# Hybrid decoder step: value products, modulation products and inverse blocks issued as one group each, bias tables made by one product, one mask a tile of probabilities, gates transposed a block at a time

## The chip, the cores and the metric

The kernel runs on one core of one Trainium2 chip. The time is the device time of one execution in microseconds (us); the number given for a kernel is the median of several runs. A profiled execution gives the spans and waits; its own time stands beside its span below. Engines are named as in the profile: PE is TensorE (matmul), PEld its weight loads, DVE VectorE, ACT ScalarE, POOL GpSimd, SP SyncE, which here issues almost all DMAs.

## The reference

One step of a hybrid decoder layer for a prompt of 2048 tokens and eight samples of 8 tokens, model width 1024. One input projection feeds two mixers; their outputs are joined, projected back and added to the input, and a gated feed-forward part follows. The parts that the change touches:

```python
mod = jnp.einsum('bd,de->be', jax.nn.silu(c), w_ada[i]) + b_ada[i]     # six vectors of 1024
sh1, sc1, g1, sh2, sc2, g2 = jnp.split(mod[:, None, :], 6, axis=-1)
h = _rmsnorm(x, norm_mix_w[i]) * (1 + sc1) + sh1
proj = jnp.einsum('bld,de->ble', h, w_in[i])
qkv, z, b_raw, a_raw, sq, sk, sv = _split_cols(proj, IN_SPLITS)
...
# gated DeltaNet, per chunk: T is the inverse of (A + I), A strictly lower triangular
beta = sigmoid(b_raw); g = -exp(A_log) * softplus(a_raw + dt_bias)
...
# sliding window attention, 8 heads, window 128, blocks of 128 queries and 256 keys
s = q k^T * 64 ** -0.5 + rel_bias[_t5_bucket(dist)]       # where 0 <= dist < 128
p = exp(s - m) / (sum(exp(s - m)) + exp(sink - m))
o = p @ v                                                 # keys of the block before and of this one
```

For a query block of 128, key j of the block before is inside the window only where j > i, and key j of the same block only where j <= i. So of the 256 probabilities of a row exactly 128 can differ from zero, and the kernel holds both halves in one 128x128 tile per head.

## The kernel before, in words

Matrices lie with channels on the 128 partitions and tokens along the free dimension. The big projections are done with weights and activations each split into a high and a low fp32r part, three products for one; the products of the mixers are plain float32, which the chip runs as two instructions each. The program runs these stages:

1. Start: the first modulation vectors, the norm of the first half of the tokens, the first products.
2. First input projection (`inproj(0, ...)`, `in_ps`) with a list of small tasks laid beside it: the other modulation vectors (`ada_cols`, L171 on, `ada_ps`), the bias tables (`bias_tables`, L532 on, `toep_ps`), the gates (`gates`, L449 on, `ba_ps` and `bat_ps`), norms of the second half, sums of down-projection weights.
3. The first half's mixers, chunk by chunk of 128 tokens (`mixers(0, ...)`): for each chunk the DeltaNet front part (`front`), the inverse (`levels`, L806 on, `z_ps` and `u_ps`), the state scan (`scan`) and the attention (`attend`, L970 on). Beside them the second half's input projection runs as filler.
4. Output projection and the feed-forward up projection of the first half (`op_ps`, `up_ps`), then the second half's mixers with the up projection as filler, then the sample group.
5. The rest of the feed-forward part (`uq_*`) and the down projection (`dn_ps`), some 1100 us, whose code the diff leaves alone.

The order of work: steps are generators, and `beside(steps, filler, share)` runs `share` steps of the filler for each small step. That fixes the order in which the program is traced. A scheduler with a timing model of its own then places the instructions of each engine, taking the earliest traced first where operands are ready by its model. On the chip each engine runs its list in that order. `tc.issue_after(x)` binds the instructions of a block on x's engine to stand behind x in it.

What the change touches:

- `ada_cols`: for four tiles of 128 columns, each a load of 512 KB (`wada`, six buffers) and eight matmuls on a quarter of the array's columns each, into one PSUM bank (L177 to L182).
- `gates`: for each block of up to 512 tokens, `ba_ev` is transposed 128 tokens at a time (L470), and each transposed piece is reduced at once (L471), 17 pairs in all.
- `bias_tables`: for each of eight heads, one matmul of the bias vector, repeated 128 times, with a one-hot table (L543), a copy (L545) and a store of 128 equal rows to `toep` (L546).
- `levels`: the first level's 16 products `z_ps` of 32x32 blocks (L815 to L817), one for each of four heads and four diagonal blocks. A block's matmul uses its own 32 rows and columns of the array. The blocks of `T` come by four DMAs, one a block.
- `attend`: the probabilities of four heads (`nl`) are transposed (L1023), copied by ScalarE to `pt` (L1025) and multiplied on POOL by two masks (L1028), into a tile for the block before (`C_TGT`) and one for this block (`C_TLE`). Four products (L1033) then sum both halves for the two value heads `v`, which take 64 columns of the array each. The first chunk has no block before it and makes two products.
- `early_h` borrows buffers of the mixers by their tags (L244).

## Time and profile before

| | |
|---|---|
| median of 3 runs | 2617.37 us (2616.8 to 2622.02) |
| the profiled execution's own time | 2613.15 us |
| its span in the profile | 2611.2 us |
| mean granted clock of TensorE | 0.998 |
| PE, PEld busy | 98%, 85% |
| DVE, ACT, POOL busy | 71%, 49%, 31% |
| DMA | 427.62 MB, mean 164 GB/s |

Busy times are unions: while two matmuls overlap, the time counts once. In the profile a group of instructions is named by line, engine, operation and tiles, "out<-in". A row of the timeline has the start, the length, engine, line and tiles, and xN where equal instructions in a row are merged. Matmuls overlap their neighbours, so the cost of one is read from its start to the start of the next one.

### The profile page before, as it was taken

To read this page: it belongs to the slowest core of one execution; us is meant where nothing else is said; L and a number is where in the kernel's file an instruction comes from. 1 tells how busy PE (TensorE), PEld (TensorE's weight loads), DVE (VectorE), ACT (ScalarE), POOL (GpSimd) and SP (SyncE) were. 2 spreads that over 40 slices of the span, in tenths; PEclk is the share of its full clock that TensorE was granted. 3 is DMA by queue.
4 is the path that set the end of the run, shared out by engine and by line. 5 is a ranking of instruction groups with operands and counts; after the bars stand their busy time and mean duration, and the time that the engine had idled before them with its cause. 6 is when DMAs were issued, how large, how long until landed. Compare 5 with 4: busy or idle time off the path is not lost.

```text
span 2611.2 us, 45384 instructions
## 1 busy us (share of the span) xinstructions
PE 2546.3 (98%) x16424; PEld 2213.2 (85%) x16424; DVE 1841.7 (71%) x3632; ACT 1290.2 (49%) x3139; POOL 802.5 (31%) x712
## 2 busy tenths in 40 slices
PE   6999999999999999999999999999999999999998
PEld 5677888888888787777777789999999998888998
DVE  6375579897543687888768674886777677687676
ACT  5464365554343454455444353554555554454453
POOL 2064243334232422223121123335655520021022
PEclk9999999999999999999999999999999999999999
DMA  7787554343556353343336357424555548676454
GB/s 275 252 293 265 154 152 118 104 116 91 126 172 207 112 154 85 98 110 95 90 107 207 122 192 221 139 69 157 172 169 179 181 146 299 206 248 200 141 191 136
DMA packets 315820, 427.62 MB, mean 164 GB/s; under 512 B 82211, under 2 KB 206212, under 8 KB 315332
## 3 DMA queue, kind: packets, MB, share of 16 engines
q1 hardware_dynamic: 315308, 423.61, 51.1%
q8 instruction: 129, 2.11, 0.3%
q0 software_dynamic: 288, 1.11, 0.1%
q14 instruction: 95, 0.78, 0.1%
HBM read 305.07 MB, written 120.57 MB: 163 GB/s over the span
## 4 chain that ended last, share of the span: by engine, by line
PE 76%; DVE 9%; DMA 7%; POOL 3%; issue 2%; ACT 2%; SPq 1%; POOLq 0%; DVEq 0%; ACTq 0%
PE up_ps L365 19%; PE dn_ps L1834 17%; PE in_ps L365 12%; PE op_ps L365 4%; PE uq_b L1616 4%; PE uq_c L1616 2%; PE uq_u L1616 2%; PE uq_g L1616 2%; PE pv_ps L1033 1%; DVE ev L573 1%; PE uq_a L1616 1%; PE as_ps L996 1%; PE u_ps L811 1%; DMA rawu<-in_w_upT_dram 1%; PE z_ps L811 1%
## 5 line engine op out<-in xcount | busy, mean ns | idle before, releaser
L365 PE MATMUL in_ps<-hi,w_hi 128*128 128x512 f32 (+2 forms) x880 | 317.7, 364 | 5.5 <-DVE ev L629 2.4
L365 PE MATMUL up_ps<-hi,w_hi 128*128 128x512 f32 (+2 forms) x808 | 314.5, 389 | 1.5 <-ACT sg L568 1.5
L365 PE MATMUL in_ps<-lo,w_hi 128*128 128x512 f32 (+2 forms) x880 | 313.8, 357 | 1.8 <-DVE lo L297 1.5
L365 PE MATMUL up_ps<-lo,w_hi 128*128 128x512 f32 (+2 forms) x808 | 313.3, 388 | 1.9 <-DVE lo L297 1.9
L365 PE MATMUL in_ps<-hi,w_lo 128*128 128x512 f32 (+2 forms) x880 | 314.2, 357 | 0.0
L365 PE MATMUL up_ps<-hi,w_lo 128*128 128x512 f32 (+2 forms) x808 | 311.6, 386 | 0.0
L1834 PE MATMUL dn_ps<-tl,wh 128*128 128x512 f32 (+2 forms) x796 | 271.5, 341 | 0.0
L1834 PE MATMUL dn_ps<-th,wh 128*128 128x512 f32 (+2 forms) x796 | 269.9, 341 | 0.0
L1834 PE MATMUL dn_ps<-th,wl 128*128 128x512 f32 (+2 forms) x796 | 268.8, 341 | 0.0
L357 DVE TENSOR_TENSOR w_lo<-w_raw,w_hi 128x1024 fp32r<-128x1024 f32 x115 | 145.0, 1261 | 86.1 <-ACT w_hi L356 81.2
L356 ACT CAST w_hi<-w_raw 128x1024 fp32r<-128x1024 f32 x126 | 132.1, 1048 | 139.9 <-PE op_ps L365 55.5
L365 PEld LDWEIGHTS in_ps<-hi,w_hi 128*128 128x128 f32 x880 | 165.1, 188 | 31.4 <-issue 8.6
L365 PEld LDWEIGHTS up_ps<-lo,w_hi 128*128 128x128 f32 x808 | 152.4, 189 | 37.3 <-issue 10.7
L365 PEld LDWEIGHTS in_ps<-lo,w_hi 128*128 128x128 f32 x880 | 165.5, 188 | 21.2 <-issue 3.8
L365 PEld LDWEIGHTS up_ps<-hi,w_hi 128*128 128x128 f32 x808 | 152.1, 188 | 35.8 <-issue 8.6
L365 PEld LDWEIGHTS in_ps<-hi,w_lo 128*128 128x128 f32 x880 | 165.3, 188 | 17.8 <-issue 3.6
L365 PEld LDWEIGHTS up_ps<-hi,w_lo 128*128 128x128 f32 x808 | 152.2, 188 | 31.3 <-issue 5.3
L1718 ACT CAST wh<-wr 128x512 fp32r<-128x512 f32 x149 | 92.3, 619 | 158.9 <-PE dn_ps L1834 105.0
L573 DVE SCALAR_TENSOR_TENSOR ev<-rb,cw,ev 128x512 f32<-128x512 f32 (+2 forms) x180 | 141.1, 789 | 38.9 <-ACT ev L566 35.5
L1834 PEld LDWEIGHTS dn_ps<-tl,wh 128*128 128x128 f32 x796 | 150.5, 189 | 15.3
L1834 PEld LDWEIGHTS dn_ps<-th,wl 128*128 128x128 f32 x796 | 150.5, 189 | 15.3
L1834 PEld LDWEIGHTS dn_ps<-th,wh 128*128 128x128 f32 x796 | 150.2, 189 | 15.4
(569 smaller groups left out, 6520.6 us busy)
## 6 DMA issues: line engine op xcount, KB each, us to landing
w_raw<-in_w_upT_dram SPq DMA_DIRECT2D x50, 512.0 KB
wada<-in_w_ada_dram SPq DMA_DIRECT2D x48, 512.0 KB
w_raw<-in_w_inT_dram SPq DMA_DIRECT2D x44, 512.0 KB
wr<-ws_d SPq DMA_DIRECT2D x88, 256.0 KB
w_raw<-in_w_outT_dram SPq DMA_DIRECT2D x34, 512.0 KB
d<-act_d SPq DMA_DIRECT2D x33, 512.0 KB
wr<-in_w_downT_dram SPq DMA_DIRECT2D x66, 256.0 KB
proj<-ev SPq DMA_DIRECT2D x44, 256.0 KB
```

What stands on the lines that cost most here:

```text
L356: nc.scalar.copy(hi, raw)
L357: (eng or nc.vector).tensor_tensor(lo, raw, hi.bitcast(F32), ALU.subtract)
L365: nc.tensor.matmul(ps[:, :n], a[:, k, :], b[:, k, :n], start=first is not False and k == ks[0] and i == 0, stop=last is not False and k == ...
L573: nc.vector.scalar_tensor_tensor(out, src(j), w[:, j:j + 1], out, ALU.mult, ALU.add)
L811: mm = lambda out, a, b, r, c: nc.tensor.matmul(out, a, b, start=True, stop=True, tile_position=(r, c))
L996: nc.tensor.matmul(banks[v][:, 256 * g:256 * g + 256 - P * k0], qs[:, 2 * (g0 + g) + v], t[:, v, :2 - k0].rearrange("p w j -> p (w j)"), s ...
L1033: nc.tensor.matmul(pv_ps[64 * v:64 * v + 64, :], (vprev[0], vt)[half][:, 64 * v:64 * v + 64], PT[v, half], start=half == k0, stop=half == 1)
L1616: nc.tensor.matmul(bk[t][:, :nb], u[:, k], v[:, k], start=new and k == 0 and y == 0, stop=k == KG - 1 and y == 2, skip_group_check=True)
L1718: nc.scalar.copy(h, raw)
L1834: nc.tensor.matmul(acc[m, s][:, :n], w[q, i][a][:, c], th[b][:, v], start=new and i == 0 and y == 0, stop=i == KH - 1 and y == 2, skip_gro ...
```

## The change

- `ada_cols`: where a group's weights aren't loaded yet, all four loads are issued first, and the products run from the last tile to the first. A new helper `behind` binds all later matmuls of the group behind its first.
- `gates`: all transposes of a block go to one PSUM bank, side by side; one reduction takes the whole tiles of a block, one more the short last tile.
- `bias_tables`: the bias vectors of eight heads are repeated 16 times each instead of 128 times, so one matmul gives 16 equal rows for every head; one copy; each store writes every row eight times.
- `levels`: the first level's products run from the last block to the first within a head, all bound behind the first one written.
- `attend`: the tile for the block before is not masked. The sum over both blocks is written as unmasked probabilities times the old values plus the probabilities masked by `C_TLE` times the difference of new and old values (`dv`, made on POOL). So POOL does one multiply a tile and one small subtraction a chunk. The four products are written from this block to the one before and from value head 1 to 0, bound behind the first. The buffers are two `pt` and two `PT` instead of one and four, and one `he` for the difference.

```diff
+    def behind(latest):
+        return tc.issue_after(latest[0]) if latest else nullcontext()
...
         ps = bank("ada_ps")
-        for q, (comp, kt) in enumerate(tiles):
-            wt = loaded[q] if loaded else ada_load(comp, kt, wpool)
+        latest = []
+        wts = loaded or [ada_load(*t, wpool) for t in tiles]
+        for q in range(len(tiles)) if loaded else range(len(tiles) - 1, -1, -1):
             for k in range(KT):
                 g = k % 4
-                nc.tensor.matmul(ps[32 * g:32 * g + 32, P * q:P * q + P], cT[:, k, :], wt[:, k, :],
-                                 start=k < 4, stop=k >= 4, tile_position=(0, 32 * g))
+                with behind([] if loaded else latest):
+                    mm = nc.tensor.matmul(ps[32 * g:32 * g + 32, P * q:P * q + P], cT[:, k, :], wts[q][:, k, :],
+                                          start=k < 4, stop=k >= 4, tile_position=(0, 32 * g))
+                latest.append(mm.ins)
...
-            for t in range(0, n, P):
+            for i, t in enumerate(range(0, n, P)):
                 rows = min(P, n - t)
-                nc.tensor.transpose(ps[:rows, t:t + 32], ev[:32, t:t + rows], cst[:32, C_ID:C_ID + 32])
-                nc.vector.tensor_reduce(ba[:rows, j, :], ps[:rows, t:t + 32].rearrange("p (a r) -> p r a", r=16)[:, 0:8],
-                                        mybir.AxisListType.X, ALU.add)
-                j += 1
+                nc.tensor.transpose(ps[:rows, 32 * i:32 * i + 32], ev[:32, t:t + rows], cst[:32, C_ID:C_ID + 32])
+            for i, m, rows in ((0, n // P, P), (n // P, 1, n % P)):
+                if rows:
+                    v = ps[:rows, 32 * i:32 * i + 32 * m].rearrange("p (j a r) -> p j r a", a=2, r=16)[:, :, 0:8]
+                    nc.vector.tensor_reduce(ba[:rows, j:j + m, :], v, mybir.AxisListType.X, ALU.add)
+                    j += m
...
-        rx = pool.tile([33, 8, P], F32, tag="relx", name="relx")
+        rx = pool.tile([33, 8, P // 8], F32, tag="relx", name="relx")
...
+        ps = bank("toep_ps", "sc")
+        nc.tensor.matmul(ps[:, :TOEP], rx.rearrange("p h r -> p (h r)"), oh, start=True, stop=True)
+        ev = gw.tile([P, 512], F32, tag="cv", name="toep_ev", bufs=CV)[:, :TOEP]
+        nc.scalar.copy(ev, ps[:, :TOEP])
         for h in range(8):
-            ps = bank("toep_ps", "sc")
-            nc.tensor.matmul(ps[:, :TOEP], rx[:, h, :], oh, start=True, stop=True)
-            ev = gw.tile([P, 512], F32, tag="cv", name="toep_ev", bufs=CV)[:, :TOEP]
-            nc.scalar.copy(ev, ps[:, :TOEP])
-            nc.sync.dma_start(toep[h], ev)
+            rows = slice(P // 8 * h, P // 8 * h + P // 8)
+            nc.sync.dma_start(toep[h].rearrange("(a r) j -> r a j", a=8), ev[rows].unsqueeze(1).broadcast_to([P // 8, 8, TOEP]))
             yield True
...
         z = flat(st_bank("z_ps"), 16)
+        latest = []
         for h in range(H):
-            for g, r in enumerate(blk):
-                mm(z[r, 0, h], AT[r, h, r], diag[g][:, h, 0:BS], 32 * g, 32 * g)
+            for g, r in reversed(list(enumerate(blk))):
+                with behind(latest):
+                    latest.append(mm(z[r, 0, h], AT[r, h, r], diag[g][:, h, 0:BS], 32 * g, 32 * g).ins)
...
+        tle = cst[:, C_TLE:C_TLE + P].unsqueeze(1).broadcast_to([P, 4, P])
+        if not k0:
+            dv = pool.tile([P, 4, P], F32, tag="he", name="dv", bufs=1)[:, 0]
+            nc.gpsimd.tensor_tensor(dv, vt, vprev[0], ALU.subtract)
...
-            pt = pool.tile([P, 4, P], F32, tag="pt", name="pt", bufs=1)
-            nc.scalar.copy(pt, heads(pt_ps))
-            for half in range(k0, 2):
-                PT[v, half] = pool.tile([P, 4, P], F32, tag="PT", name="PT", bufs=4)
-                nc.gpsimd.tensor_tensor(PT[v, half], pt, tri[half], ALU.mult)
+            PT[v, 0] = pool.tile([P, 4, P], F32, tag="pt", name="pt", bufs=2)
+            PT[v, 1] = pool.tile([P, 4, P], F32, tag="PT", name="PT", bufs=2)
+            nc.scalar.copy(PT[v, 0], heads(pt_ps))
+            nc.gpsimd.tensor_tensor(PT[v, 1], PT[v, 0], tle, ALU.mult)
             yield True
         pv_ps = bank("pv_ps", "at")
-        for half in range(k0, 2):
-            for v in range(2):
-                nc.tensor.matmul(pv_ps[64 * v:64 * v + 64, :], (vprev[0], vt)[half][:, 64 * v:64 * v + 64],
-                                 PT[v, half], start=half == k0, stop=half == 1)
+        latest = []
+        for half in range(1, k0 - 1, -1):
+            for v in (1, 0):
+                with behind(latest):
+                    mm = nc.tensor.matmul(pv_ps[64 * v:64 * v + 64, :],
+                                          (vprev[0], vt if k0 else dv)[half][:, 64 * v:64 * v + 64],
+                                          PT[v, half], start=half == 1, stop=half == k0)
+                latest.append(mm.ins)
```

The order that the scheduler writes, at three places. On PE in the second chunk of the first half's mixers, the kernel before; pv_ps are the value products, in_ps is the filler's projection and u_ps belongs to the inverse:

```order
L365 MATMUL in_ps<-hi,w_lo 128x384
L1033 MATMUL pv_ps<-PT,vt 64x512
L365 MATMUL in_ps<-hi,w_hi 128x384
...
L1033 MATMUL pv_ps<-PT,vt 64x512 x2
L365 MATMUL in_ps<-lo,w_hi 128x384
...
L1033 MATMUL pv_ps<-PT,vt 64x512
L811 MATMUL u_ps<-inv_2253,Y 32x32 x8
```

On PE in the same chunk of the changed kernel, where dv is the difference of values and pt the unmasked tile:

```order
L373 MATMUL in_ps<-lo,w_hi 128x384
L1050 MATMUL pv_ps<-PT,dv 64x512 x2
L1050 MATMUL pv_ps<-pt,vt 64x512 x2
L373 MATMUL in_ps<-hi,w_lo 128x384
L373 MATMUL in_ps<-hi,w_hi 128x384
```

The four products stood at three places with filler between them and stand at one now.

On PE in the kernel before, the inverse's first level of a later chunk (z_ps; uu_ps is a product of the scan, as_ps scores of the attention):

```order
L365 MATMUL in_ps<-hi,w_hi 128x384
L811 MATMUL z_ps<-T_2255,AM 32x16
L871 MATMUL uu_ps<-vb,inv_2254 128x128
L811 MATMUL z_ps<-T_2255,AM 32x16
L871 MATMUL uu_ps<-vb,inv_2254 128x128
L811 MATMUL z_ps<-T_2255,AM 32x16
L871 MATMUL uu_ps<-vb,inv_2254 128x128
L811 MATMUL z_ps<-T_2255,AM 32x16 x13
```

On PE in the changed kernel, the same level of the same chunk:

```order
L373 MATMUL in_ps<-hi,w_hi 128x384
L884 MATMUL uu_ps<-vb,inv_2220 128x128 x4
L1012 MATMUL as_ps<-kh,qs 128x256
L1012 MATMUL as_ps<-kl,qs 128x256
L822 MATMUL z_ps<-T_2221,AM 32x16 x16
L1012 MATMUL as_ps<-kh,qs 128x256
```

The 16 block products stood in four pieces between the scan's products and stand in one piece behind them.

On PE in the kernel before, a stretch of the first projection; ada_ps are modulation products, toep_ps bias products, ba_ps and bat_ps belong to the gates, and adat_ps are transposes of modulation vectors:

```order
L365 MATMUL in_ps<-hi,w_hi 128x512
L181 MATMUL ada_ps<-wada,cT 32x128 x6
L543 MATMUL toep_ps<-oh,relx 128x384
L181 MATMUL ada_ps<-wada,cT 32x128 x25
L543 MATMUL toep_ps<-oh,relx 128x384
L181 MATMUL ada_ps<-wada,cT 32x128
L365 MATMUL in_ps<-lo,w_hi 128x512
```

On PE in the changed kernel, the group of modulation products that stands nearest to it, and the gates' transposes of one block:

```order
L373 MATMUL in_ps<-hi,w_lo 128x512
L188 MATMUL ada_ps<-wada,cT 32x128 x32
L373 MATMUL in_ps<-hi,w_hi 128x512
L373 MATMUL in_ps<-lo,w_hi 128x512
L373 MATMUL in_ps<-hi,w_lo 128x512
L478 MATMUL bat_ps<-cst,ba_ev 128x32 x4
```

A group of 32 is in one piece, no bias product stands inside it, and the four transposes of a block follow each other. Counted over the whole order, unbroken runs of pv_ps go from 39 to 17, of z_ps from 73 to 49, of ada_ps from 29 to 19, of bat_ps from 17 to 5, and of toep_ps from 8 to 1.

More of the change, by code (lines that the diff above doesn't have):

```diff
@@ L6 @@
-from contextlib import ExitStack
+from contextlib import ExitStack, nullcontext
 import numpy as np
@@ L244, in early_h @@
         room = iter(spare("xz") + spare("qs", 1, 2) + spare("kh") + spare("kl") + spare("u") + spare("o")
-                    + spare("nl", 3) + spare("nl", 3) + spare("nl", 3) + spare("pt") + [spare("PT", 4)[0] for _ in range(4)])
+                    + spare("nl", 3) + spare("nl", 3) + spare("nl", 3) + [spare(t, 2)[0] for t in ("pt", "pt", "PT", "PT")] + spare("he"))
         for i, t in enumerate(room):
@@ L536, in bias_tables @@
         nc.sync.dma_start(rb[0:32], I["rel_bias"])
[L537 removed]
+        rx = pool.tile([33, 8, P // 8], F32, tag="relx", name="relx")
         oh = pool.tile([33, TOEP], F32, tag="oh", name="oh")
         nc.sync.dma_start(oh, I["consts"][:33, C_OH:C_OH + TOEP])
[L540 to L546 removed]
+        nc.vector.tensor_copy(rx, rb.unsqueeze(2).broadcast_to([33, 8, P // 8]))
+        ps = bank("toep_ps", "sc")
+        nc.tensor.matmul(ps[:, :TOEP], rx.rearrange("p h r -> p (h r)"), oh, start=True, stop=True)
+        ev = gw.tile([P, 512], F32, tag="cv", name="toep_ev", bufs=CV)[:, :TOEP]
+        nc.scalar.copy(ev, ps[:, :TOEP])
+        for h in range(8):
+            rows = slice(P // 8 * h, P // 8 * h + P // 8)
+            nc.sync.dma_start(toep[h].rearrange("(a r) j -> r a j", a=8), ev[rows].unsqueeze(1).broadcast_to([P // 8, 8, TOEP]))
             yield True
@@ L985, in attend @@
         yield True
-        tri = [cst[:, t:t + P].unsqueeze(1).broadcast_to([P, 4, P]) for t in (C_TGT, C_TLE)]
+        tle = cst[:, C_TLE:C_TLE + P].unsqueeze(1).broadcast_to([P, 4, P])
+        if not k0:
+            dv = pool.tile([P, 4, P], F32, tag="he", name="dv", bufs=1)[:, 0]
+            nc.gpsimd.tensor_tensor(dv, vt, vprev[0], ALU.subtract)
         nl = [pool.tile([P, 4, P], F32, tag="nl", name="nl", bufs=3) for _ in range(2)]
```

1 line of the change is left out of this document (removed).

## The prediction

> **What bounds the kernel now.** I read the page first, for busy times and the chain, then the table of busy time by stage, then the timeline of TensorE at the places that the change touches, and last the waits. In the page, look at PE's share, at the granted clock, and at who holds the chain.
>
> ```profile
> span 2611.2 us, 45384 instructions
> PE 2546.3 (98%) x16424; PEld 2213.2 (85%) x16424; DVE 1841.7 (71%) x3632; ACT 1290.2 (49%) x3139; POOL 802.5 (31%) x712
> PEclk9999999999999999999999999999999999999999
> PE 76%; DVE 9%; DMA 7%; POOL 3%; issue 2%; ACT 2%; SPq 1%; POOLq 0%; DVEq 0%; ACTq 0%
> ```
>
> TensorE is busy for 2546.3 of 2611.2 us, idle for 64.9; the granted clock reads 9, 90% or more, in every slice. In the table by stage (length, then busy time of PE, PEld, DVE, ACT, POOL, then clock and DMA share), the start loses 20 us of that and the rest is nearly gapless:
>
> ```profile
> 0.00:65.00 65.00, 44.73 (x410) 33.86 (x411) 44.14 (x110) 33.59 (x59) 14.41 (x15) 1.00 0.77 276
> 65.00:196.00 131.00, 127.76 (x993) 94.50 (x992) 74.28 (x113) 70.79 (x156) 43.32 (x35) 1.00 0.76 272
> 392.00:588.00 196.00, 194.44 (x1648) 172.44 (x1647) 173.49 (x523) 112.92 (x393) 64.69 (x67) 1.00 0.40 113
> 979.00:1371.00 392.00, 387.99 (x2841) 302.50 (x2840) 308.19 (x797) 198.32 (x607) 97.22 (x83) 1.00 0.36 98
> ```
>
> So time taken off TensorE between 65 and 1371 us comes off the end, as long as VectorE (173.5 of 196 us in the first mixer stage) and DMA (share 0.76 in the first projection) keep up. After the sample group's mixers the two kernels issue the same rows in the same order; that part only moves forward. The prediction is a sum of TensorE time, in terms of "visits": a visit is an unbroken run of matmuls of one PSUM tile.
>
> **Value products.** One chunk of attention before, on TensorE (start, length, line, tiles; x4 is two products, since each float32 product is two instructions):
>
> ```profile
> 438.50 0.33 PE L365 MATMUL in_ps<-hi,w_lo 128*128 128x384 f32 x1
> 438.67 0.34 PE L365 MATMUL in_ps<-hi,w_hi 128*128 128x384 f32 x1
> 438.94 1.08 PE L1033 MATMUL pv_ps<-PT,vt 128*64 128x512 f32 x4
> 439.95 0.45 PE L365 MATMUL in_ps<-lo,w_hi 128*128 128x384 f32 x1
> 440.23 0.34 PE L365 MATMUL in_ps<-hi,w_lo 128*128 128x384 f32 x1
> ...
> 440.87 1.07 PE L1033 MATMUL pv_ps<-PT,vt 128*64 128x512 f32 x2
> 441.87 0.35 PE L811 MATMUL u_ps<-inv,Y 32*32 32x32 f32 x10
> ```
>
> A later chunk with three products in one visit, and the weight loads of all visits (min, median, max in ns):
>
> ```profile
> 702.18 1.93 PE L1033 MATMUL pv_ps<-PT,vt 128*64 128x512 f32 x6
> 704.04 0.41 PE L365 MATMUL in_ps<-hi,w_hi 128*128 128x320 f32 x1
> ```
>
> ```profile
> L1033 PEld LDWEIGHTS pv_ps<-PT,vt x124: 132/136/137, 385.4 to 1336.4; 128*64 128x64 f32 x124
> ```
>
> Lengths overlap, so cost is from start to next start. Two products for the two halves of the array cost 1.01 us (438.94 to 439.95), one alone 1.00 (440.87 to 441.87): the second rides free. Three in one visit, a pair and one, cost 1.86, so what follows without a break adds 0.85. A chunk before is mostly alone, pair, alone: 3.01 us in three visits. The changed order has all four in one visit, two pairs: 1.01 + 0.01 + 0.85 = 1.87. Before has 39 visits: nine chunks of three, five of two (1.00 + 1.86), one with its four products in one visit but in the order alone, pair, alone (1.01 + 2 x 0.85 = 2.71), and the first chunk, whose two products follow each other (1.00 + 0.85) and now pair (1.01). Gain: 9 x 1.14 + 5 x 0.99 + 0.84 + 0.84 = 16.9 us.
>
> A rule speaks against the 1.87: the Trainium skill, "TensorE: Matmul & The Clock Gate", Part 3, The mechanism, says that a weight load overlaps running matmuls only where the row group differs, and all four products use all rows. By it the second pair would wait for two loads of 0.136 us, 0.27 a chunk, and the sum would be 4.1 us smaller over 15 chunks. The visit of three has just such a follower, and its 0.85 holds whatever the loads cost; a solitary product, loads and array change included, costs 1.00. So the trace gives no room for 0.27 more, and the 0.85 stands.
>
> **Breaks.** The same rows price a break of the projection's stream. Its matmuls of 384 columns start 0.17 us apart (438.50, 438.67). The last one ahead of the visit takes 0.27 until the visit starts, the first one behind it 0.28 (439.95 to 440.23): 0.10 + 0.11 = 0.21 us beyond the visit's own time. From the order of the two kernels, visits fall from 39 to 17 (pv_ps), 73 to 49 (z_ps), 29 to 19 (ada_ps), 17 to 5 (bat_ps), 8 to 1 (toep_ps): 75 fewer. All at 0.2 make 15.0 us. Where a visit stood among other small products, leaving it restores no stream; if that held for all 36 of z_ps and bat_ps, 39 would be left and 7.8 us. In the chunk shown next the extra visits do break the stream. I take 13, ends 8 and 15.
>
> **Inverse blocks.** z_ps of the first level, in four visits and, in another chunk, in one:
>
> ```profile
> 674.00 0.23 PE L811 MATMUL z_ps<-T,AM 32*32 32x16 f32 x2
> 674.16 0.44 PE L365 MATMUL in_ps<-hi,w_lo 128*128 128x384 f32 x1
> ...
> 676.48 0.42 PE L811 MATMUL z_ps<-T,AM 32*32 32x16 f32 x26
> 676.83 0.44 PE L365 MATMUL in_ps<-lo,w_hi 128*128 128x384 f32 x1
> ```
>
> ```profile
> 468.88 0.44 PE L811 MATMUL z_ps<-T,AM 32*32 32x16 f32 x32
> 469.25 0.44 PE L365 MATMUL in_ps<-lo,w_hi 128*128 128x384 f32 x1
> ```
>
> Three of 0.16 and one of 0.35 against 0.37: 0.46 us for three visits less, 0.15 each; 24 visits make 3.7 us. Ends: 2.5 (some small visits hold two products already) and 3.7.
>
> **Modulation, gates, bias tables.** In the first projection, a bias product, a group of modulation products split by a gates transpose, and a group of 64 in one piece:
>
> ```profile
> 82.72 0.91 PE L543 MATMUL toep_ps<-oh,relx 33*128 33x384 f32 x2
> 83.56 0.50 PE L365 MATMUL in_ps<-hi,w_hi 128*128 128x512 f32 x1
> ```
>
> ```profile
> 140.38 0.86 PE L181 MATMUL ada_ps<-wada,cT 128*32 128x128 f32 x24
> 141.17 0.24 PE L470 MATMUL bat_ps<-cst,ba_ev 32*128 32x32 f32 x1
> 141.35 1.02 PE L181 MATMUL ada_ps<-wada,cT 128*32 128x128 f32 x24
> 142.30 0.50 PE L365 MATMUL in_ps<-lo,w_hi 128*128 128x512 f32 x1
> ```
>
> ```profile
> 163.97 1.95 PE L181 MATMUL ada_ps<-wada,cT 128*32 128x128 f32 x64
> 165.85 0.50 PE L365 MATMUL in_ps<-hi,w_lo 128*128 128x512 f32 x1
> ```
>
> A bias product costs 0.84 (82.72 to 83.56); seven fewer are 5.9 us. Their ScalarE copies go too, off the path (ACT 49% busy). The table stores stay eight and as large; they come at once, and the mixers, the next stage, read them. An ada_ps group in one visit is 64 in 1.88 us, 0.029 each; the split one does 48 in 0.79 + 0.95 = 1.74 where 48 x 0.029 = 1.41: 0.33 for a split, ten splits 3.3 us (ends 1 and 3.3). A gates transpose is 0.18 in a visit of its own; four in one cost between 0.18 and 4 x 0.18, so twelve visits less give 0 to 2.2, and I take the middle, 1.1. The eleven or so reductions fewer on VectorE cost nothing on TensorE.
>
> **Sum of work:** 16.9 + 13 + 3.7 + 5.9 + 3.3 + 1.1 = 43.9 us of TensorE; by the low ends 16.9 + 8 + 2.5 + 5.9 + 1 + 0 = 34.3, by the high ones 16.9 + 15 + 3.7 + 5.9 + 3.3 + 2.2 = 47.0.
>
> **Waits.** The change ties each group behind its first product, the one whose operand comes last: the last masked tile of POOL, the last block's load, the last of four modulation weights. While that one waits, all of TensorE's queue waits behind it, the projection first. What waited there before (line, releaser, sum, times, longest), and POOL's row:
>
> ```profile
> PE z_ps L811 <- DVE T L832: 2.0, 2, 1.2
> PE pv_ps L1033 <- POOL PT L1028: 1.6, 2, 1.0
> PE ada_ps L181 <- DMA wada<-in_w_ada_dram: 0.6, 1, 0.6
> ```
>
> ```profile
> L1028 POOL TENSOR_TENSOR PT<-pt,cst 128x512 f32<-128x512 f32 x62 | 87.2, 1427 | 110.0 <-ACT pt L1025 110.0
> ```
>
> Only 4.2 us in five waits, so the written order fits the chip well. POOL now does one multiply a tile instead of two: 30 x 1.43 = 43 us less, and the last tile is ready after two multiplies (2.9 us) instead of four (5.7). The 15 differences of values are small and early on an engine that is 31% busy. The modulation weights are asked for in fours on SyncE's queue, where projection weights stand behind them. Bounds: 1.6 us less than before, if POOL is never late again; a wait of 1.0, pv_ps's longest, at each of 40 groups (16 of pv_ps, 16 of z_ps, 8 of ada_ps), 40 us more. I take 4 more, as much again as stood there, since the nearest rows are those five waits.
>
> **Time.** 43.9 - 4 = 39.9 us. The profiled execution took 2613.15 us (span 2611.2 and 1.95 around it), so 2573 by its own measure; the median of the runs, 2617.37, lies 4.2 above, and 2617.4 - 39.9 = 2577.
>
> **Rivals.**
>
> DMA takes the first stage's gain. From 65 to 196 us go 5.9 + 3.3 + 0.6 and 23 breaks or so, 4.6: 14.4 us. The same bytes in less time put the share from 0.76 to 0.85 on average, and bursts of four weight tiles stand in one queue. If weights come late there, all 14.4 return: 2591. Against it: TensorE was held up for only 3.2 us in that stage. Chance 0.12.
>
> VectorE takes the mixers' gain. A chunk loses about 2 us of TensorE time (1.1 of products, 0.2 of blocks, 3 breaks), 7.5 us from 392 to 588, where VectorE goes from 173.5 of 196 (89%) to 173.5 of 188.5 (92%). If its queue holds back all eight chunks of the first half, 16 us return: 2593. Against: 15 us are left there, and the second half has 308 of 392 (79%). Chance 0.09.
>
> The joining does not do what it says: the groups of pv_ps and z_ps are now written in falling order of array column, before in rising order, as in all rows above. If pairs overlap only when they rise, a group costs 1.00 + 3 x 0.85 = 3.55 instead of 3.01, so 15 x 0.54 = 8 us more in place of 16.9 less: 2577 + 25 = 2602. Chance 0.04; nothing in the rows depends on direction.
>
> One bank, four row groups: if matmuls of different rows could not write one PSUM bank together, each of 16 block products would cost a visit of 0.16, 2.56 instead of 0.83, 28 us more and 3.7 not gained: 2609. The Trainium skill states such a rule, "TensorEngine Tiling (Array Packing)", Gotcha 1: PSUM Pressure. By that rule z_ps could not be joined; the row at 468.88, 32 in 0.37 us, disagrees. Chance 0.01.
>
> The ties make it slower. Each of the 40 groups gives on average 43.9 / 40 = 1.1 us; if its first product waits longer than that on average, the kernel loses, since nothing behind it on TensorE may pass. At 2 us each, 80 us: 2617.4 + 36 = 2653. For it: a written order decides here, and the longest waits were 1.0 and 1.2. Against: five waits in the 141 visits that the three tiles made. Chance 0.06.
>
> **Chances.** Forecast 0.68, its own range 2566 (47 of work, and 4 less waiting than before) to 2591 (34.3 of work, 8 of waits). DMA 0.12 and VectorE 0.09 lie at 2591 and 2593. The range 2563 to 2600 takes in these three and leaves out the last three rivals, 0.11, and tails. A change under 0.2% (5.2 us) cannot be told from none. Of the last rival 0.05 are slower; 0.03 in all go to mixtures that end within 0.2%. Faster 0.92, same 0.03, slower 0.05.
>
> **What would show it.** pv_ps in 16 or 17 visits of about 1.87 us; PE busy down by some 43 us, its idle time near 65; toep_ps once; no wait on PT or wada in the list above 2 us. Wrong if PE's idle time grows by over 20 us (then look for ada_ps at 65 to 196, for VectorE at 392 to 783, or for pv_ps and z_ps behind their first product), or if four products take over 2.2 us.

## The result and the profile after

The changed kernel takes 2591.95 us (median of five runs, 2587.97 to 2596.04), the kernel before 2616.80 in the five runs beside it (2614.74 to 2622.02). The ratio is 0.9901, 95% interval 0.9887 to 0.9915: 24.9 us faster, where the forecast was 39.9. That is inside the range of 2563 to 2600 and just past the slow end of the forecast's own, 2591. The profiled execution took 2595.62 us, its span 2593.8.

The changed kernel's page: span, busy times, and the chain of waits by engine.

```profile
span 2593.8 us, 45288 instructions
PE 2519.9 (97%) x16410; PEld 2212.9 (85%) x16410; DVE 1811.2 (70%) x3621; ACT 1281.8 (49%) x3132; POOL 758.3 (29%) x697
PE 69%; DVE 11%; DMA 10%; ACT 3%; issue 3%; POOL 2%; SPq 1%; DVEq 0%; POOLq 0%; ACTq 0%
```

TensorE's busy time fell by 26.4 us and not by some 43, and its idle time rose from 64.9 to 73.9. In the chain, DVE and DMA grew from 9% and 7% to 11% and 10%. The same four stretches as before (length, busy PE, PEld, DVE, ACT, POOL, granted clock, DMA share):

```profile
0.00:65.00 65.00, 44.78 (x410) 33.87 (x411) 44.16 (x110) 33.32 (x57) 14.52 (x15) 1.00 0.78 276
65.00:196.00 131.00, 121.13 (x980) 94.26 (x979) 70.68 (x107) 67.37 (x150) 44.22 (x35) 0.97 0.79 279
392.00:588.00 196.00, 188.45 (x1652) 171.96 (x1653) 170.44 (x520) 114.10 (x401) 58.36 (x65) 1.00 0.42 116
979.00:1371.00 392.00, 389.48 (x2942) 310.14 (x2941) 302.08 (x830) 206.31 (x638) 76.89 (x77) 1.00 0.40 111
```

From 65 to 196 us TensorE is idle for 9.9 us (3.2 before) and its granted clock is 0.97 (1.00 before). From 392 to 588 it is idle for 7.6 us (1.6 before). What the change was to do, it does. One chunk's value products on TensorE (start, length, line, tiles):

```profile
437.59 1.08 PE L1050 MATMUL pv_ps<-PT,dv 128*64 128x512 f32 x4
438.50 1.03 PE L1050 MATMUL pv_ps<-pt,vt 128*64 128x512 f32 x4
439.46 0.44 PE L373 MATMUL in_ps<-hi,w_lo 128*128 128x384 f32 x1
```

Four products cost 439.46 - 437.59 = 1.87 us, the forecast to the hundredth, and so they do in 13 of the 15 chunks; one chunk still has two visits, and one takes 3.41 us at half the clock. These are waits of TensorE in the changed kernel (line, releaser, sum, times, longest):

```profile
PE rb_ps L230 <- DVE dg L226: 4.8, 4, 2.6
PE ada_ps L188 <- DMA wada<-in_w_ada_dram: 4.5, 3, 2.0
...
PE u_ps L822 <- DVE Y L872: 3.0, 1, 3.0
PE ss_ps L222 <- POOL xacc L318: 2.9, 2, 2.7
PE z_ps L822 <- DVE T L864: 2.7, 2, 1.4
...
PE pv_ps L1050 <- POOL PT L1043: 2.1, 3, 1.4
PE d_ps L727 <- ACT junk L711: 2.0, 1, 2.0
```

And these are waits of the kernel before:

```profile
PE rb_ps L222 <- DVE dg L218: 4.2, 4, 1.7
...
PE u_ps L811 <- DVE Y L859: 3.2, 2, 2.9
...
PE p_ps L884 <- DVE xz L942: 2.2, 2, 1.9
```

New are the waits at ss_ps for POOL, at z_ps for the T of L864 and at d_ps. The one at ada_ps grew from 0.6 us, and the longest at rb_ps from 1.7 to 2.6. The one at u_ps is not new: the kernel before has it at the same place, 2.9 us long.

Behind the longest waits stands something that the kernel before, its last 10 us aside, shows at one place only: stretches in which the granted clock is exactly half. Four of eight such stretches (the last numbers: clock, DMA share, GB/s):

```profile
106.51:109.92 3.41, 3.41 (x43) 2.31 (x34) 0.00 (x0) 0.58 (x1) 0.00 (x0) 0.50 1.03 399
147.47:150.88 3.41, 3.41 (x10) 2.76 (x10) 1.33 (x5) 1.10 (x2) 0.86 (x1) 0.50 1.00 375
...
608.27:615.10 6.83, 6.35 (x25) 6.24 (x26) 6.53 (x26) 0.85 (x2) 0.00 (x0) 0.50 0.46 137
...
1075.89:1079.31 3.42, 3.42 (x10) 0.77 (x8) 3.32 (x17) 1.75 (x5) 2.87 (x3) 0.50 0.00 0
```

Each is 3.41 us long or twice that, and each follows a gap: the 2.0 us at ada_ps, the 2.7 at ss_ps, the 3.0 at u_ps, the 2.0 at d_ps. Work takes about twice as long there (in the kernel of gaps below, matmuls start 0.43 us apart in such a stretch and 0.23 elsewhere), so TensorE counts as busy while it loses, by an estimate from half the clock, 1.71 us in 3.41. That is why busy time alone misleads here. I split the span in three: idle time (span less PE's busy time), 1.71 us for each half-clock window, and the rest, work at full clock. Records of the clock begin 22 to 25 us into the span; the half clock at the very end, which every kernel has, is left with the work. Each ratio is to runs of the kernel before taken beside it.

| kernel | median, us | ratio to before, 95% | PE busy | idle | half-clock windows | work | mean clock of its runs |
|---|---|---|---|---|---|---|---|
| before | 2614.5 to 2616.8 | 1 | 2546.3 | 64.9 | 1 | 2544.6 | 0.995 (52 runs) |
| the change | 2591.95 | 0.9901 (0.9887 to 0.9915) | 2519.9 | 73.9 | 9 | 2504.5 | 0.993 |
| the change, again | 2590.33 | 0.9907 (0.9892 to 0.9922) | 2516.3 | 71.3 | 9 | 2500.9 | 0.993 |
| mixers' parts | 2588.36 | 0.9902 (0.9887 to 0.9917) | 2521.6 | 64.4 | 4 | 2514.8 | 0.995 |
| first projection's parts | 2623.42 | 1.0036 (1.0023 to 1.0049) | 2546.1 | 74.2 | 7 | 2534.1 | 0.993 |
| without modulation groups | 2585.86 | 0.9894 (0.9876 to 0.9911) | 2512.6 | 71.5 | 5 | 2504.1 | 0.993 |
| value products | 2592.75 | 0.9915 (0.9895 to 0.9935) | 2529.6 | 59.8 | 4 | 2522.8 | 0.996 |
| products reversed only | 2616.81 | 1.0007 (0.9996 to 1.0018) | 2536.7 | 75.0 | 5 | 2528.2 | 0.993 |
| modulation groups only | 2629.93 | 1.0054 (1.0033 to 1.0075) | 2554.1 | 70.9 | 5 | 2545.6 | 0.994 |
| bias tables only | 2612.00 | 0.9987 (0.9977 to 0.9997) | 2546.2 | 61.5 | 6 | 2535.9 | 0.994 |
| mask only | 2611.91 | 0.9982 (0.9970 to 0.9995) | 2548.0 | 57.8 | 4 | 2541.2 | 0.995 |
| values, blocks, bias | 2589.12 | 0.9900 (0.9884 to 0.9916) | 2522.5 | 66.2 | 9 | 2507.1 | 0.994 |
| the change, share 2.2 | 2589.00 | 0.9897 (0.9879 to 0.9915) | 2512.8 | 75.8 | 8 | 2499.1 | 0.992 |

Columns from PE busy to work are of one profiled execution each, and two of the same kernel (the change and its repeat) differ by 3.6 us in work and 2.6 in idle time. The last column is the mean over a kernel's timed runs. The profiled execution of before, with one window and a clock of 0.998, lies at the top of what the runs of before show, 0.991 to 0.998; the mean of 52 is 0.9953. Luck is part of that: windows at half clock lie in a raster of 3.41 us, and in this profile a line of it cuts the 2.9 us at u_ps into 1.6 and 1.3, and a wait of 2.4 us at in_ps into 1.5 and 0.9. Neither is followed by half a clock. In the changed kernel the same wait at u_ps is cut into 2.5 and 0.5, and one is. So the profiled pair overstates the clock's part. By the runs, the change's nine with a mean of 0.9930, it is (1 - 0.9930) x 2591 less (1 - 0.9953) x 2616: 18.1 - 12.3 = 5.8 us.

### The profile page after: what moved, and what is told of

It reads as the page before. It is cut to its first block, busy times and chain, and to the rows that moved or that the text cites. A ratio compares the mean times of both kernels' runs of the same rounds, so it can differ in the third digit from the quotient of the medians.

```text
span 2593.8 us, 45288 instructions
## 1 busy us (share of the span) xinstructions
PE 2519.9 (97%) x16410; PEld 2212.9 (85%) x16410; DVE 1811.2 (70%) x3621; ACT 1281.8 (49%) x3132; POOL 758.3 (29%) x697
## 4 chain that ended last, share of the span: by engine, by line
PE 69%; DVE 11%; DMA 10%; ACT 3%; issue 3%; POOL 2%; SPq 1%; DVEq 0%; POOLq 0%; ACTq 0%
PE up_ps L373 18%; PE dn_ps L1853 15%; PE in_ps L373 9%; PE op_ps L373 5%; PE uq_b L1635 4%; DVE ev L584 3%; PE uq_c L1635 2%; PE uq_u L1635 2%; PE uq_g L1635 2%; DMA suv<-in_w_downT_dram 2%; PE uq_a L1635 1%; PE pv_ps L1050 1%; PE as_ps L1012 1%; DMA mt<-mixd 1%; DMA rawu<-in_w_upT_dram 1%
## 5 line engine op out<-in xcount | busy, mean ns | idle before, releaser
L364 ACT CAST w_hi<-w_raw 128x1024 fp32r<-128x1024 f32 x126 | 132.1, 1048 | 144.2 <-PE op_ps L373 59.8
L1853 PEld LDWEIGHTS dn_ps<-tl,wh 128*128 128x128 f32 x796 | 150.5, 189 | 16.4 <-DVE tl L1738 1.1
```

Source lines behind the costliest of these rows:

```text
L364: nc.scalar.copy(hi, raw)
L1853: nc.tensor.matmul(acc[m, s][:, :n], w[q, i][a][:, c], th[b][:, v], start=new and i == 0 and y == 0, stop=i == KH - 1 and y == 2, skip_gro ...
```

## Experiments

My theory was: the work went off TensorE as summed, and part of it came back as idle time and half-clock windows, above all in the first projection. The rivals: the loss lies in the mixers; every part is simply smaller than priced.

**The mixers' parts alone.** The kernel before with the edits to `levels` and `attend` (and the buffers of `early_h` that they need):

```diff
+            for g, r in reversed(list(enumerate(blk))):
+                with behind(latest):
...
+            nc.gpsimd.tensor_tensor(PT[v, 1], PT[v, 0], tle, ALU.mult)
...
+        for half in range(1, k0 - 1, -1):
+            for v in (1, 0):
```

> Only the mixers' parts of the change: joined value products with one mask, and joined inverse blocks. Theory (work saved as summed, eaten mostly in the first projection, where tied modulation groups wait and TensorE then runs windows of 3.4 us at half clock): PE visits of pv_ps 39 to 17 and of z_ps 73 to 49, 16.9 + 3.7 + 46 x 0.17 = 28 us of work off TensorE at full clock, 4 us more idle, two or three half-clock windows more (1.7 us each): 20 us faster than before, 2597 (2593 to 2601), nearly all that the whole change gives. Rival one (the loss lies in the mixers: ties behind the first product): no more than 12 us faster, 2605. Rival two (each part simply gives 25/40 of its price, no place for the loss): 28 x 25/40 = 17 us faster, 2600, with TensorE's work down by only 17 and no new half-clock windows.

Measured 2588.36, 26.1 us faster, and 29.8 us of work less in the profile where 28 was priced; idle time unchanged. These parts carry all that the whole change gives, and more than the 20 us that I expected of them.

**The first projection's parts alone.** The edits to `ada_cols`, `gates` and `bias_tables`, nothing of the mixers:

```diff
+        wts = loaded or [ada_load(*t, wpool) for t in tiles]
+        for q in range(len(tiles)) if loaded else range(len(tiles) - 1, -1, -1):
...
+        rx = pool.tile([33, 8, P // 8], F32, tag="relx", name="relx")
...
+                nc.tensor.transpose(ps[:rows, 32 * i:32 * i + 32], ev[:32, t:t + rows], cst[:32, C_ID:C_ID + 32])
```

> Only the first projection's parts of the change: modulation groups tied and loaded by fours, one bias product, gates transposed a block at a time. Theory: 5.9 + 3.3 + 1.1 + 29 fewer visits x 0.17 = 15 us of work off TensorE, but about 7 us more idle between 65 and 261 us (ada_ps waiting for wada) and four half-clock windows there, 7 us: within 4 us of before, 2613 to 2617. Rival one (the loss lies in the mixers): 12 to 15 us faster, 2603. Rival two (every part at 25/40): 9 us faster, 2608, without new half-clock windows.

Measured 2623.42: 9 us slower, worse than the theory had it. Work fell by 10.5, idle time rose by 9.3, and six windows were added. In the profiled pair the loss is in a stage that none of these edits touches. From the first in_ps to the first u_ps the kernel has 12.6 us less work, 5.4 more idle time and 5.1 lost to the clock, and is 2.1 us shorter, much as the theory had it. From there to the first op_ps, the first half's mixers, it is 10.8 us longer: 3.2 of work, 5.9 of idle time, 1.7 of the clock. The written order came out with 79 visits of z_ps instead of 73 and 40 of pv_ps instead of 39; that the scheduler began that stage from another state is my reading, not shown.

**Without the modulation groups.** The whole change, with `ada_cols` as before:

```diff
-        wts = loaded or [ada_load(*t, wpool) for t in tiles]
-        for q in range(len(tiles)) if loaded else range(len(tiles) - 1, -1, -1):
+        for q, (comp, kt) in enumerate(tiles):
+            wt = loaded[q] if loaded else ada_load(comp, kt, wpool)
...
```

> The whole change without the tied modulation groups (their loads and products stand as before). In the written order ada_ps has 20 visits against the whole change's 19, so the ties save almost no visit that the other parts did not save. Theory (the loss lies in the first projection, by the tied groups' wait for their four loads): the two waits on wada (1.4 and 2.0 us) and one to three half-clock windows go, 4 to 8 us faster than the whole change, 2584 to 2588. Rival one (the loss lies in the mixers): like the whole change, 2590 to 2594. Rival two (half-clock windows come with the higher share of work, not with gaps): like the whole change, with as many windows between 65 and 261 us as it has.

Measured 2585.86, the lowest median of the study, within what the theory expected. But its interval overlaps that of the whole change, so the 4.5 us between them are not settled. Work is that of the whole change: the joined groups save nothing that the other parts had not saved.

**The change again.** No edit.

> The whole change unaltered, for a second profile. If half-clock windows are decided by how a gap of TensorE lies within the chip's own 3.41 us raster, the same gaps (2.0 to 2.7 us between 100 and 245 us) throttle in part this time, not all the same ones: 4 to 9 windows, the execution's time moving by 1.7 us a window, between 2588 and 2596. If they belong to the instructions at those places, the same eight windows at the same instructions. Rival (they are noise of this chip, unrelated to gaps): windows at places without a gap over 1.3 us.

Measured 2590.33. Nine windows again, in part behind other gaps. Those behind ss_ps, rb_ps, up_ps and d_ps came back. The one at ada_ps did not, since that gap was 1.1 us this time; and at op_ps a gap of 2.1 us had none, where the first profile has one behind 1.7 us. A line of the raster cuts the 2.1 into 1.6 and 0.6. So the window goes with the gap and its place in the raster, not with the instructions.

**Value products alone.** The edits to `attend` only.

```diff
+            dv = pool.tile([P, 4, P], F32, tag="he", name="dv", bufs=1)[:, 0]
+            nc.gpsimd.tensor_tensor(dv, vt, vprev[0], ALU.subtract)
...
+        for half in range(1, k0 - 1, -1):
+            for v in (1, 0):
```

> Only the value products of the change: joined, unmasked tile times old values, one mask, difference of values. Theory (in the mixers the terms of the sum hold): 16.9 us and 22 visits fewer at 0.2, 21 us of work off TensorE, 3 us more of waits for PT and of shifted stalls: 18 us faster than the kernel before on the same chip, ratio 0.993; the mixers' parts together gave 26. Rival (the value products were oversized and the inverse blocks carried the mixers' gain): 10 us or less, ratio 0.996 or more.

Measured 2592.75, 22.7 us faster; work down by 21.8 where 16.9 + 22 x 0.17 = 20.7 was priced. The inverse blocks are the rest of the mixers' gain, 8 us of work (2522.8 to 2514.8; priced 3.7 + 24 x 0.17 = 7.8) and 3 to 4 us of time.

**Reversed order alone.** Both masks stay; two lines change:

```diff
-        for half in range(k0, 2):
-            for v in range(2):
+        for half in range(1, k0 - 1, -1):
+            for v in (1, 0):
...
-                                 PT[v, half], start=half == k0, stop=half == 1)
+                                 PT[v, half], start=half == 1, stop=half == k0)
```

> The kernel before with one edit: the four value products written in reversed order (this block first, value head 1 first). Both masks stay, so POOL still does two multiplies a tile and there is no difference of values. In the written order pv_ps has 19 visits against 39. Theory (the gain is TensorE's order, the mask only brings the last tile earlier): nearly the gain of the value products' part, 13 to 19 us faster, ratio 0.993 to 0.995, with waits of pv_ps for PT up by 3 to 5 us since the first product waits for POOL's fourth multiply. Rival (without the single mask the joined group waits for POOL at every chunk, about 1 us and a half-clock window at some): 5 us faster or less, ratio 0.998.

Measured 2616.81: no gain at all. My theory fell here, and the rival held. TensorE's work did fall by 16.4 us, as joining should make it. Its waits between 307 and 1340 us, of this kernel:

```profile
PE pv_ps L1033 <- POOL PT L1028: 5.5, 4, 1.7
PE u_ps L811 <- DVE Y L859: 5.4, 4, 2.3
PE p_ps L884 <- DVE xz L942: 3.6, 3, 1.8
```

And the same waits with the single mask (value products alone):

```profile
PE u_ps L816 <- DVE Y L864: 2.8, 2, 1.9
...
PE pv_ps L1042 <- POOL PT L1035: 1.4, 1, 1.4
...
PE p_ps L889 <- DVE xz L947: 0.6, 1, 0.6
```

With two masks the three waits make 14.5 us, with one mask 4.8, in the kernel before 7.0. Idle time over the whole span is 75.0 against 59.8 with one mask and 64.9 before, and the mean clock 0.9932 against 0.9960 with one mask, which is 7 us more. The loss is in the second half. Up to the first op_ps the reversed order is 6.2 us ahead of the kernel before, against 8.0 for the value products alone; from there to the first uq_ product it falls 6.1 back, with 11.4 us more idle time, where the value products gain 13.9. The waits for POOL's tile lie mostly in the first half (4.3 of 5.5), those at u_ps and p_ps, for VectorE, in the second (8.8 of 9.0). So it is not shown that the one causes the other. By the times, the single mask with its buffers, which alone changes little on TensorE (work 2541.2 against 2544.6), is what makes the joining pay.

**The mask alone.** The edits of the value products, with the four products in their old order:

```diff
-        for half in range(1, k0 - 1, -1):
-            for v in (1, 0):
+        for half in range(k0, 2):
+            for v in range(2):
```

> Only the mask of the change, without the joining: one multiply a tile, difference of values, the buffers as in the change, but the four products written in the order of the kernel before. In the written order pv_ps has 35 visits against 39 before and 17 in the change. Reversing the products alone had saved 16 us of TensorE's work and lost as much to idle time and half-clock windows; both edits together gained 23. Theory (the mask takes POOL's second multiply out of the way of the joined group, and has no work of its own on TensorE): alone 0 to 4 us faster, ratio 0.9985 to 1.000, TensorE's work down by about 1 us. Rival (the mask itself is what gains, since POOL or a port that it shares with VectorE holds up the mixers): 10 us or more, ratio under 0.996, idle time down by that much.

Measured 2611.91, 4.6 us faster, a little beyond the theory's 4 and far from the rival's 10. So joining alone gives nothing, the mask alone 5, both 23: the two belong together.

**Modulation groups alone.** The edit to `ada_cols` only, as shown in the second experiment.

> Only the modulation groups of the change: four loads issued first, products from the last tile to the first. The written order has 27 visits of ada_ps against 29, since transposes of the gates and bias products still split groups. Theory (the joined groups are what lost in the first projection): 1 us of work less, 3 to 5 us of waits on wada and one or two half-clock windows more: 3 to 7 us slower, ratio 1.001 to 1.003. Rival (any part that shortens the first projection just moves its stalls): no change, ratio 0.9995 to 1.0005.

Measured 2629.93, 14.5 us slower, twice the most that I had thought. No work is saved (2545.6 against 2544.6). Two details make no difference. With the loads first but the products in rising order, the written order is that of the kernel before; and without the bindings of `behind`, that of the whole change stays what it is, row for row. So it is the reversed order of the products that acts. In the profiled pair, 6.6 us of the loss stand from the first in_ps to the first u_ps, and 6.9 in the first half's mixers, which this edit does not touch. The first part can be followed in SyncE's queue (start, length, transfers), modulation groups only:

```profile
164.51 0.80 SPq L173 DMA_DIRECT2D wada<-in_w_ada_dram  x2
165.36 2.34 SPq L315 DMA_DIRECT2D xst<-in_xT_dram  x5
...
177.14 0.33 SPq L356 DMA_DIRECT2D w_raw<-in_w_inT_dram  x1
```

The same place of the kernel before:

```profile
153.55 1.02 SPq L168 DMA_DIRECT2D wada<-in_w_ada_dram  x1
154.62 3.36 SPq L307 DMA_DIRECT2D xst<-in_xT_dram  x5
...
165.03 0.33 SPq L348 DMA_DIRECT2D w_raw<-in_w_inT_dram  x1
```

The last modulation loads start 11 us later, the second half's tokens for the norm (`xst`, which may not be issued ahead of them) 10.7 later, and the next projection weight 12. The norm then comes late to TensorE (waits from 65 to 275 us):

```profile
PE rb_ps L230 <- DVE dg L226: 7.1, 4, 4.1
```

In the kernel before that wait was 2.5 in all, the longest 1.5. That the late loads cause this wait is read from the queue and not tried by itself; what made the mixers longer is not known, but their written order has 75 visits of z_ps instead of 73.

**Bias tables alone.** The edit to `bias_tables` only.

```diff
+        nc.tensor.matmul(ps[:, :TOEP], rx.rearrange("p h r -> p (h r)"), oh, start=True, stop=True)
...
+            nc.sync.dma_start(toep[h].rearrange("(a r) j -> r a j", a=8), ev[rows].unsqueeze(1).broadcast_to([P // 8, 8, TOEP]))
...
```

> Only the bias tables of the change: one product and one copy for eight heads. Work: 5.9 us of products, 8 + 4 visits fewer of toep_ps and ada_ps, 2.4: 8 us off TensorE in the first projection. Theory (the modulation groups are what lost there): 5 to 8 us faster, ratio 0.997 to 0.998. Rival (the first projection's end is held by chains on POOL, VectorE and DMA, so TensorE only waits longer for sums, for norms and for its first operands of the mixers): idle time and half-clock windows before 307 us grow by as much, no change or slower, ratio 0.9995 to 1.002.

Measured 2612.00, 3.5 us faster, between theory and rival. Work fell by 8.7 where 8 was priced; in the profiled pair, the first projection (first in_ps to first u_ps) lost 7.1 us of work but is as long as before (283.4 us against 283.5), with 1.9 more idle and three windows, 5.1.

**Value products, blocks and bias tables.** The whole change without its edits to `ada_cols` and `gates`.

```diff
-            for i, t in enumerate(range(0, n, P)):
+            for t in range(0, n, P):
...
```

> The whole change without the modulation groups and without the gates' block transposes: value products, inverse blocks and bias tables only. In the written order ada_ps has 25 visits and bat_ps 17. Theory (the parts of the mixers and the bias product carry the gain; what shortens the side tasks further only sends TensorE into waits earlier): 26 + 3 = 29 us faster than the kernel before, ratio 0.989, as good as the whole change without the modulation groups or better. Rival (the gates' transposes have their 3.5 us of gain there too): 25 us, ratio 0.9905.

Measured 2589.12, 27.4 us faster. It lies between the theory and its rival, and its interval holds both; the gates' transposes can't be told from nothing.

**More projection between the side tasks.** The whole change and one number:

```diff
-    SHARE = (5.4, 5.5, 4.0, 2.05, (2.0, 1.4), 5.0, (1.3, 2.0), 8.0)
+    SHARE = (5.4, 5.5, 4.0, 2.2, (2.0, 1.4), 5.0, (1.3, 2.0), 8.0)
```

> The whole change, with 2.2 steps of the projection for each small side task of the first projection in place of 2.05. Theory (the side tasks have become lighter on TensorE, so they come to their sums before POOL and VectorE have them, 2.7 us at ss_ps and 2.6 at rb_ps; 7% more projection between them gives 5 us by the first place and 9 by the second): the waits of ss_ps for POOL and of rb_ps for VectorE fall under 1.2 us each, two of the four half-clock windows before 260 us go, 5 to 7 us faster than the whole change, ratio to before 0.988. Rival (DMA bounds the stage: whatever comes later waits as long): idle time before 307 us stays at 18 us and the time at that of the whole change, ratio 0.991.

Measured 2589.00: not told apart from the whole change. By the ratios it is 1 to 3 us faster, where the theory had 5 to 7; the interval holds theory and rival. Its waits from 65 to 275 us:

```profile
PE kq_ps L708 <- DMA kq<-proj: 5.3, 1, 5.3
PE ada_ps L188 <- DMA wada<-in_w_ada_dram: 3.3, 2, 2.0
PE ss_ps L222 <- POOL xacc L318: 2.4, 2, 1.3
PE rb_ps L230 <- DVE dg L226: 2.0, 2, 1.8
```

The waits that I meant to shorten did shorten, from 2.9 to 2.4 and from 3.1 to 2.0, and a wait for the mixers' first operands, which go through DRAM, grew from 1.6 to 5.3. In this profile the gaps that closed opened again further on.

**Gaps and the clock.** A kernel of its own, the loop in short:

```python
for k in range(n):                                  # 84 to 124 matmuls
    nc.tensor.matmul(ps[k % 2], w, x if y is None else y, start=k < 2, stop=k >= n - 2)
...
nc.vector.scalar_tensor_tensor(y, ps[(n - 1) % 2], 0.0, x.bitcast(F32), ALU.mult, ALU.add)
nc.vector.tensor_copy(big[:, :2], y[:, :2].bitcast(F32))
nc.vector.tensor_scalar_add(big[:, :cols], big[:, :cols], 1.0)     # 64 to 3840 columns
nc.vector.tensor_copy(y[:, :2], big[:, cols - 2:cols])
```

> A kernel of its own that computes nothing of the reference: 60 dense runs of 84 to 124 projection-like matmuls (128x512, some 0.23 us apart, 19 to 28 us a run), and between two runs one gap of TensorE, in which VectorE works for a length that is stepped from about 1 to at least 3 us, in mixed order, so that gaps fall anywhere in the raster. Theory (TensorE's clock is halved for one window of 3.41 us behind each window of a fixed 3.41 us raster in which it idled for over about half, 1.65 to 1.85 us, as the twelve traces have it): no half-clock window behind a gap under 1.6 us; behind a longer gap g with a chance of 1 - (2 x 1.75 - g) / 3.41, that is 0.5 at 1.8 us, 0.7 at 2.5, 0.85 at 3.0, all at 3.5; every miss is a gap that a raster line cuts into two parts under 1.85. Each such window costs 1.7 us. Rival one: only a gap that fills a whole window throttles: none under 3.4 us. Rival two: the clock follows load or the tied groups' instructions and not gaps: half-clock windows at no fixed place.

Measured: 59 gaps of 1.45 to 3.48 us, 32 of them followed by a half-clock window, two of these by two. Cut by the raster into windows of 3.41 us, all 26 gaps whose largest part is 1.873 us or less pass at full clock, and all 31 of 1.906 or more throttle the next window; between lie two, at 1.879 (throttled) and 1.880 (not). Three gaps, in windows of that raster (length, busy PE, PEld, DVE, POOL, clock):

```profile
470.26:473.67 3.41, 1.63 (x8) 1.08 (x7) 1.49 (x4) 0.00 (x0) 1.00 0.00 0
473.67:477.08 3.41, 3.41 (x16) 2.78 (x16) 0.00 (x0) 0.00 (x0) 1.00 0.00 0
1610.31:1613.72 3.41, 1.43 (x7) 0.88 (x6) 1.69 (x4) 0.00 (x0) 1.00 0.00 0
1613.72:1617.14 3.42, 3.42 (x10) 2.65 (x9) 0.00 (x0) 0.00 (x0) 0.50 0.00 0
739.91:743.32 3.41, 1.54 (x7) 0.94 (x5) 1.76 (x3) 0.00 (x0) 1.00 0.00 0
743.32:746.74 3.42, 1.94 (x8) 1.61 (x9) 1.39 (x2) 0.00 (x0) 1.00 0.00 0
746.74:750.15 3.41, 3.41 (x16) 2.81 (x15) 0.00 (x0) 0.00 (x0) 1.00 0.00 0
```

A window with 1.78 us idle is followed by one at full clock (16 matmuls), one with 1.98 by one at half (10). The third gap is the longest of the three, 3.35 us, but the raster cuts it in 1.87 and 1.48, and nothing follows. The theory held, with its threshold at 1.9 rather than 1.75; the rivals are out. The full kernels agree on one side: in their 13 traces, from 65 us on, all 38 raster windows with over 1.9 us of idle time are followed by a window at half clock. On the other side they go further than this kernel: of the 47 with 1.5 to 1.85 us, 16 are, and 13 of their 70 windows at half clock (the end of the span left out) stand behind less than 1.5 us. Eight of these 13 are the second window of a double stretch. In the kernel of gaps a second one came where 0.60 and 1.28 us of a gap fell into the window that was already at half clock, and none where 0.53 us or less did; so less idle time seems to keep the clock down than to bring it down. In the full kernels it is 0.16 to 1.16 us. What halves the clock in the other cases is open.

## Why the prediction was right, and where not

- **The sum of work** (43.9 us): right within the spread of two profiles, which have 40.1 and 43.7. Value products 20.7 priced with their breaks, 21.8 measured; inverse blocks 7.8 and 8.0; bias tables 5.9 and 11 visits at 0.17, 7.8, against 8.7. The first projection's parts alone have 10.5 where some 15 were priced, so the shortfall, as far as there is one, is there. Four products cost 1.87, so the follow-on price of 0.85 held.
- **The split term of the modulation** (3.3 us): put to the wrong cause. The splits go because the bias products and the gates' transposes no longer stand inside the groups; without the change to `ada_cols` there are 20 visits, with it 19. By itself the reversed order costs 14.5 us, and a cost of it was in no term; no run shows a gain of it.
- **Waits** (4 us, bounds -1.6 to 40): too small. Idle time rose by 9.0 and 6.4 us in the profiles, and by more over the runs: 24.9 us of gain, 5.8 lost to the clock and some 42 of work leave 11 for it. The step that failed is that only "those five waits" were counted. At these three places the forecast was good: for the T of L832, for PT and for wada TensorE waited 4.2 us before, and 8.7 and 8.3 after. But waits came at places that no term had, 2.9 us at ss_ps for POOL, 2.7 at z_ps for the T of L864, 2.0 at d_ps. My reading is that TensorE comes sooner to work whose operands come no sooner; no run delays or hastens one of these operands alone. And "the written order fits the chip well" was true of the old order only. By stage, idle time and clock took back 11.6 us in the first projection and 10.3 in the first half's mixers (15.3 and 7.1 in the repeat), and little elsewhere.
- **The clock**: no term had it. The row of nines and the mean of 0.998 were read as full clock for good; that the raster cut two of the longest gaps in that profile was luck. By their mean clocks the runs lose 12.3 us to half clock before and 18.1 after, the end of the span included.
- So of the 15 us between 39.9 and 24.9, some 7 are the idle time beyond 4, 6 the clock and 2 the work. The idle part is what the others leave, and the profiles show less of it.
- **POOL's second mask**: rightly named as what lets the last tile come after two multiplies; but its worth was in no number. Without it the joined products gain nothing (2616.81).
- **What would show it**: of the signs named, the 17 visits of pv_ps, their 1.87 us and the single toep_ps product came. PE's busy time fell by 26 us and not by 43, its idle time is 73.9 and 71.3 and not near 65, and the waits for PT and wada sum to 2.1 and 4.5 us.
- **DMA takes the first stage's gain** (2591): the time came out so, and the place too. The first projection up to the first u_ps took 283.5 us before, and 283.3 and 285.9 after, with 11.8 and 12.9 us less work. But the weights' transfers are one cause of four: in the profile of after, waits for them there went from nothing to 3.4 us, ss_ps for POOL from nothing to 2.9, rb_ps from 2.5 to 3.1, and the clock took 6.8. The DMA share went to 0.79 and not to 0.85.
- **VectorE takes the mixers' gain**: no, the mixers' parts gave 26 us. **Reversed order doesn't pair** and **one bank, four row groups**: no, 1.87 us and 0.37 us a visit. The Trainium skill's rule of one bank for one row tile ("TensorEngine Tiling (Array Packing)", Gotcha 1: PSUM Pressure) would have made 16 block products take 2.56 us by the prediction's working; in these traces the four row groups share a bank, and the 16 take 0.37 us. **The ties make it slower**: for the modulation groups the written order is the same without the ties, but their reversed order does make it slower, alone by 14.5 us; for the other two groups, no.

## What to carry to other kernels

Work taken off a bound engine is worth what is left after the waits that appear with it; list the operands that come from elsewhere behind each saving, since in this kernel five versions with 2499 to 2515 us of work all end within 2586 to 2592. Where TensorE is nearly full, price a gap of more than 1.9 us at its length and up to 1.7 us more, and take the clock of many runs, not of one profile. An edit that joins products and one that brings their last operand earlier belong together, and a reversed loop must be judged by the whole written order that comes of it, the loads and the stages behind it included.

## What the runs showed of the hardware

In these runs TensorE's clock was halved for a whole window of 3.41 us each time it had idled for over about 1.9 us, 55%, of the window before (31 of 31 in the kernel of gaps, 38 of 38 in the full kernels). In dense streams of matmuls less did not do it (26 of 26 at 1.873 us or less); in the full kernels it sometimes did, for a cause that stays open. The raster does not start with the program: its first line in the records of the full kernels lies anywhere from 22.1 to 25.4 us after the span's start. Gaps of the same length count or not by where a line of the raster cuts them. The Trainium skill, "TensorE: Matmul & The Clock Gate", Part 1, What's actually happening, has that free-running window of 3413 ns and the half rate, and the runs agree. Its table puts the half rate behind at least one idle window of some 3.4 us, and its rule in HAM oscillation asks for no gap over that; here gaps of 1.9 to 2.7 us were enough, and a gap of 3.35 us was not.

The version without the modulation groups is the fastest measured (2585.86, ratio 0.9894). It beats the kernel before; that it beats the whole change is likely by its median and not shown.
